# Two-layer hybrid decoder trunk on one core: the two channel blocks of each norm sum and layer norm sum are added on VectorE ahead of the product with the constant matrix

## The chip, the cores and the metric

The kernel runs on 1 core of one Trainium2 chip. The metric is device time in microseconds (us); lower is better. The engines are TensorE (PE in the profile, its weight loads PEld), VectorE (DVE), ScalarE (ACT), GpSimd (POOL) and SyncE (SP, which issues most DMAs).

## The reference

One sequence of 528 positions (512 and 16 meta tokens) with 1024 channels passes two layers. All arithmetic is float32. In each layer:

```python
def rms_norm(x, g):
    y = x * lax.rsqrt(jnp.mean(x * x, axis=-1, keepdims=True) + RMS_EPS)
    return y * g

def layer_norm(x, g, b):
    mu = jnp.mean(x, axis=-1, keepdims=True)
    var = jnp.mean(jnp.square(x - mu), axis=-1, keepdims=True)
    return (x - mu) * lax.rsqrt(var + LN_EPS) * g + b

def mixer_sublayer(h, ...):
    u = rms_norm(h, pre_g)
    q, k, v, f_logit, a_val, a_gate, sc_b, sc_c, sc_x = split(u @ w_in)
    y_attn = forgetting_attention(q, k, v, log_sigmoid(f_logit + b_forget))
    a = causal_depthwise_conv(a_val * sigmoid(a_gate), a_dw_w) + a_dw_b     # 31 taps, 256 channels
    y_conv = silu(layer_norm(a, a_ln_g, a_ln_b)) @ a_pw_w
    y_sc = sc_b * causal_depthwise_conv(sc_c * sc_x, sc_conv_w)             # 3 taps, 256 channels
    y = head_rms_norm(concat([y_attn, y_conv, y_sc]), head_g) @ w_out
    return h + rms_norm(y, post_g)

def ffn_sublayer(h, ...):
    g, up = split(causal_depthwise_conv(rms_norm(h, pre_g) @ w_up, conv_w))
    return h + rms_norm((silu(g) * up) @ w_down, post_g)
```

The change touches only sums over channels: the mean of squares of `rms_norm` over 1024 channels (both the pre norms and the post norms) and the two means of `layer_norm` over 256 channels.

## The kernel before

**Layout.** Activations lie with channels on the 128 partitions and positions along the free dimension: 1024 channels are 8 blocks of 128, and the 528 positions are worked on in two halves of 264 (H). In the second layer some spans are 250 or 256 columns, since the meta tokens fall away. A sum over channels is therefore a sum over the partitions and over the blocks. TensorE makes it: a product with a 128x128 constant matrix (`om_d`, all 1/1024; `om_c`, all 1/256) adds over the partitions and leaves the mean in every partition of one PSUM bank.

**Products.** The large matrix products are split in three: each float32 operand is a rounded high part and a low part of type fp32r, and `mm3` (line 831) makes high*high, high*low and low*high. Their weights stream in by DMA, ScalarE rounds the high part and VectorE subtracts for the low part (lines 652 and 653, 641 and 642, 666 and 667, 789 and 793). The products with `om_d` and `om_c` take plain float32 operands.

**A norm sum** (class `Norms`). `square` (line 916) is called for blocks k and k + 1 together: ScalarE squares a pair of blocks of n columns, 2n in all, and for k > 0 VectorE adds the pair to the pair `acc` (line 934), which stays two blocks wide. With `apart` set, the last pairs are not added but kept as parts of their own (line 937); that is so for the pre norm that ends layer 0 (`APART` = 2, line 2431), where pairs 4 and 6 are parts. At the end of the last layer, `square_alone` (line 944) keeps the last two blocks as single parts for the second half. `factor` (line 956) is a thread: it waits for each part, takes a PSUM bank and adds both blocks of a part into it on TensorE, one product a block (line 974). Then ScalarE and VectorE make the reciprocal root from the bank (lines 984 to 998).

Norm sums stand in four places: in the opening (two halves of the first pre norm); behind the output projection of each layer (post norm of the mixer and pre norm of the feed-forward part, two halves each); at the end of layer 0 (post norm, and the pre norm of layer 1 with its parts); and at the end of layer 1 (post norm alone).

**The layer norm** (`conv_tail`, line 1748) follows the 31 taps of the convolution (VectorE, line 1153). For each half TensorE multiplies `om_c` with both channel blocks of `conv` (line 1760), VectorE subtracts the mean (line 1764), ScalarE squares into `sq` (line 1766), TensorE multiplies `om_c` with both blocks of `sq` (line 1789), and `rsq` (line 1278) makes the factor.

**What sets the order.** A planner, `Flow` (line 253), writes each engine's instruction order by hand in the stretches around the mixers and the output norms. It keeps an estimated clock for each engine; operations carry an estimated duration, what they wait for, and a priority (a lower number goes first among those that are ready). TensorE's work consists of threads: generators that yield what they wait for, of which the first that is ready goes on. `flow.mm(us)` advances TensorE's estimated clock, and `mm4_us(264)` is 0.445 us for a float32 product, `dve_us(264)` 0.437 us for a VectorE operation. So each engine runs its queue in the planned order, whatever the true durations are. While `conv_tail` waits, TensorE's other threads are projections (`fill`), row maxima (`maxima`), exponentials and attention norms. In the feed-forward part the order is that of the program, and TensorE runs products (lines 837 and 2288) throughout.

Of the kernel before, what the change touches and what calls it, by code (L numbers as in the profile page):

```python
# [21 lines left out]
H = L // 2  # L22
# [25 lines left out]
LN_EPS = 1e-5  # L48
# [313 lines left out]
def mm4_us(n):  # L362

    return max(n / 600 + 0.005, 0.22)


def act_us(n):
    return 0.17 + 0.0009 * n


def dve_us(n):
    return 0.17 + 0.00101 * n
# [17 lines left out]
def tile_hybrid_trunk(ctx: ExitStack, tc: tile.TileContext, xT, wflat, pv_d, out):  # L390
    nc = tc.nc
# [58 lines left out]
    def const_mat(name, val, dt=F32):  # L450
        t = T(const, [P, P], dt, name)
        mset(t, val)
        return t
# [6 lines left out]
    om_c = const_mat("om_c", 1.0 / 256)  # L460
# [21 lines left out]
    flow = Flow()  # L482
# [5 lines left out]
    def half_sl(hf):  # L488
        return slice(H * hf, H * (hf + 1))
# [29 lines left out]
    sums = {}  # L519
# [172 lines left out]
    def dve(us, fn, *after, **kw):  # L692
        return flow.op("dve", us, fn, after, **kw)
# [204 lines left out]
    class Norms:  # L898
# [17 lines left out]
        def square(self, key, k, src, n, *after, prio=1):  # L916

            apart = self.alone.get(key, self.apart.get(key[0], 0))
            s = self.sums.setdefault(key, {"parts": {}})
            us = act_us(2 * n)  # L920
            box, slot = {}, Slot()

            def squares(tile):
                box["c"] = tile()
                nc.scalar.activation(box["c"], src, AF.Square)

            if k == 0:
                a = act(us, lambda: squares(lambda: T(self.pool, [P, 2, H], F32, "acc", 2)[:, :, :n]), *after,
                        prio=prio, takes=[(self.acc, slot)])
                s["acc"], s["at"] = box, a  # L930
            else:
                a = act(us, lambda: squares(lambda: self.c_tile(n)), *after, prio=prio, takes=[(self.c, slot)])
                if k < KD - 2 * apart:
                    s["at"] = dve(dve_us(2 * n), lambda: nc.vector.tensor_add(s["acc"]["c"], s["acc"]["c"], box["c"]),
                                  a, s["at"], prio=prio)
                    slot.close(s["at"])
            if k == 0 or k >= KD - 2 * apart:
                s["parts"][max(0, k // 2 - KD // 2 + apart + 1) if k else 0] = box, slot
                box["at"] = [a]
            if k == KD - 2 * apart - 2:  # L940
                s["acc"]["at"], s["acc"]["there"] = [s["at"]], True
            return a

        def square_alone(self, key, j, src, n, *after, prio=1):

# [179 lines left out]
    def mixer(l, ypool, first, close_first, spans, front, rzs, u_at):  # L1125
# [19 lines left out]
        conv, apads, gated_at, gated = front.conv, front.apads, front.at, front.gated  # L1145
# [10 lines left out]
        taps = []  # L1156
# [94 lines left out]
        def bank(kind):  # L1251

            slot = yield from flow.grab(banks[kind])
            return psum[:, slot.buf], slot
# [23 lines left out]
        def rsq(x, slot, eps, tok, prio=1):  # L1278

            mine = Slot()  # L1280
            box = {}
            us = act_us(H)
            prio = next(turns)

            def ln():
                box["r"], box["t"] = (T(mp, [P, H], F32, f"rs_{i}", 2) for i in "rt")
                nc.scalar.activation(box["r"], x, AF.Ln, bias=c_eps[eps] if eps else 0.0)

            a = act(us, ln, tok, prio=prio, takes=[(rings["rs"], mine)])
            b = act(us, lambda: nc.scalar.activation(box["r"], box["r"], AF.Exp, scale=-0.5), a, prio=prio)  # L1290
            c = act(us, lambda: nc.scalar.activation(box["t"], box["r"], AF.Square), b, prio=prio)
            d = dve(dve_us(H), lambda: nc.vector.scalar_tensor_tensor(
                box["t"], in0=x, scalar=eps, in1=box["t"], op0=ALU.add, op1=ALU.mult), c, prio=prio)
            slot.close(a, d)
            e = dve(dve_us(H), lambda: nc.vector.scalar_tensor_tensor(
                box["t"], in0=box["t"], scalar=3.0, in1=box["r"], op0=ALU.subtract, op1=ALU.mult), d, prio=prio)
            box["prio"] = prio
            return box, mine, e
# [449 lines left out]
        def conv_tail(blk):  # L1748

            w = blk.w  # L1750
            yield taps
            a2 = [ytiles(4), ytiles(5)]
            sq = [T(mq, [P, L + CK - 1], F32, "apad", 2) for _ in range(2)]
            us, vs = act_us(H), dve_us(H)
            at = {}
            for hf in range(2):
                c = half_sl(hf)
                ps, slot = yield from bank("mm")
                for j in range(2):
                    nc.tensor.matmul(ps[:, :H], lhsT=om_c, rhs=conv[j][:, c], start=j == 0, stop=j == 1)  # L1760
                tok = flow.mm(2 * mm4_us(H))
                subs = []
                for j in range(2):
                    subs.append(dve(vs, lambda j=j, ps=ps, c=c: nc.vector.tensor_sub(
                        conv[j][:, c], conv[j][:, c], ps[:, :H]), tok))
                    at[hf, j] = act(us, lambda j=j, c=c: nc.scalar.activation(sq[j][:, c], conv[j][:, c], AF.Square), subs[-1])
                slot.close(*subs)
                yield
            done = {}

            def silu(j, c, box, mine, e):
                n, s = conv[j][:, c], sq[j][:, c]
                f = dve(stt_us(H), lambda: nc.vector.scalar_tensor_tensor(
                    n, in0=n, scalar=gcol("a_ln_g", j), in1=box["t"], op0=ALU.mult, op1=ALU.mult), e)
                mine.use(f)
                g = act(us, lambda: nc.scalar.activation(s, n, AF.Exp, bias=minus_b[:, j:j + 1], scale=-1.0), f)
                g = act(us, lambda: nc.scalar.activation(s, s, AF.Ln, bias=c_one), g)
                g = act(us, lambda: nc.scalar.activation(s, s, AF.Exp, scale=-1.0), g)
                f = dve(stt_us(H), lambda: nc.vector.scalar_tensor_tensor(
                    n, in0=n, scalar=col("a_ln_b", j), in1=s, op0=ALU.add, op1=ALU.mult), g)  # L1780
                g = act(us, lambda: nc.scalar.copy(a2[j][0][:, c], n), f)
                return dve(vs, lambda: nc.vector.tensor_sub(a2[j][1][:, c], n, a2[j][0][:, c].bitcast(F32)), g)

            for hf in range(2):
                c = half_sl(hf)
                yield [at[hf, 0], at[hf, 1]]
                ps, slot = yield from bank("mm")
                for j in range(2):
                    nc.tensor.matmul(ps[:, :H], lhsT=om_c, rhs=sq[j][:, c], start=j == 0, stop=j == 1)
                box, mine, e = rsq(ps[:, :H], slot, LN_EPS, flow.mm(2 * mm4_us(H)))  # L1790
                done[hf] = [silu(j, c, box, mine, e) for j in range(2)]
                mine.close()
                yield
            yts, got = [], {}
            ends = done[0] + done[1]
            for m in range(2):
                yield ends
                yt = T(mq, [P, L], F32, "cacc", 2)
                for hf in range(2):
                    ps, slot = yield from bank("mm")  # L1800
                    mm3({hf: ps[:, :H]}, w, range(2), lambda b, k, hf: a2[k][b][:, half_sl(hf)],
                        cols=slice(P * m, P * (m + 1)))
                    tok = flow.mm(6 * mm_us(H))
                    got[m, hf] = act(us, lambda ps=ps, yt=yt, hf=hf: nc.scalar.copy(yt[:, half_sl(hf)], ps[:, :H]), tok)
                    slot.close(got[m, hf])
                    yield
                yts.append(yt)
            blk.slot.close(tok)
            for m in range(2):
                sq = T(mq, [P, L + CK - 1], F32, "apad", 2)[:, :L]  # L1810
                flow.thread(plain_head_norm(4 + m, yts[m], sq, [got[m, hf] for hf in range(2)]), True)
# [34 lines left out]
        for i, f in enumerate(sums_at(l, 1)):  # L1846
            copies, *adds = sum_steps(l, f)
            tok = flow.op("sp", 2.0, copies, (Tok(flow.pe + SUM_AT[i]),), prio=8, lat=SUM_LAT)
            for op in adds:
                tok = gp(SUM_US, op, tok, prio=8, lat=SUM_LAT)  # L1850
# [178 lines left out]
    with tc.tile_pool(name="pre", bufs=2, reuse_waits="tile") as sp, tc.manual_schedule(engines=every):  # L2029
# [13 lines left out]
        for k in range(KD):  # L2043
            hk, hi, lo, gc = h[:, k, :H], u_raw[0][k], u_raw[1][k], g0[:, k:k + 1]
            c = act(act_us(H) + 0.06, lambda hk=hk, hi=hi, gc=gc: nc.scalar.activation(hi, hk, AF.Copy, scale=gc),
                    h_at[0, k - k % 2], prio=0)
# [47 lines left out]
    for l in range(DEPTH):  # L2094
# [23 lines left out]
        with tc.tile_pool(name=f"fp{l}", bufs=2, reuse_waits="tile") as fp:  # L2118
# [226 lines left out]
            for part, nf in enumerate(PARTS):  # L2345
                for f in range(f0, f0 + nf):
# [15 lines left out]
                    for i in (2 * f, 2 * f + 1):  # L2362
# [6 lines left out]
                        ps = mmt((6, 2)[i % 2]) if ts else mmt()  # L2369
# [17 lines left out]
                if part < len(PARTS) - 1:  # L2387
# [3 lines left out]
                    for some in ((0, 1), *((m,) for m in range(2, KD))):  # L2391
                        ws = [next_w() for _ in some]
                        tiles = [mmt((4, 6, 2)[m % 3]) if seven else mmt() for m in some]
# [97 lines left out]
```

## Time and profile before

| | |
|---|---|
| runs | 1262.51, 1263.30, 1263.05 us; median 1263.05 |
| the profiled execution, first to last instruction (span) | 1262.4 us |
| mean granted TensorE clock in it | 0.999 |
| records on TensorE | 9554 matmuls |
| float32 products with `om_d` (line 974) | 84 records |
| float32 products with `om_c` (lines 1760 and 1789) | 16 + 16 records |
| HBM traffic over the span | 175 GB/s |

The profile gives the profiled execution's span; what lies around it is the rest of the measured time, 0.65 us up to the median. A row of the timeline shows the start, the length, the engine, the line, the operation with its tiles, its shape and how many such instructions follow one another; in brackets stands how long the engine was idle before it, and on which engine's instruction it waited. The lengths of matmul records overlap, so the pace of a run of matmuls is read from the chain of waits or from the starts. A row of the windows shows the stretch, its length, the busy time of TensorE, of its weight loads, of VectorE, ScalarE and GpSimd (with instructions), then the clock, the share of the DMA engines and GB/s. A row of a source view shows the shortest, median and longest duration in ns.

### The profile page before, as it was taken

The numbers are of one execution on the slowest core, as the hardware profiler recorded it, in microseconds if no ns is written. First come the engines' busy times: TensorE is split into PE (matmuls) and PEld (weight loads), VectorE is DVE, ScalarE is ACT, GpSimd is POOL, SyncE is SP. The second block draws the span as 40 slices with busy tenths as digits, with TensorE's granted clock in tenths as the row PEclk, the third lists the DMA queues.
The fourth block names the chain that finished last, engine by engine and source line by source line (L and its number), as shares of the span: only waits on it lengthen the run. The fifth ranks groups of instructions, "written<-read, shape, count | busy, mean of one in ns | idle before, by whom it ended". The sixth has DMA issues, their size and how long they took to land.

```text
span 1262.4 us, 24292 instructions
## 1 busy us (share of the span) xinstructions
PE 1243.7 (99%) x9554; PEld 1194.0 (95%) x9554; DVE 926.1 (73%) x1581; ACT 710.3 (56%) x1377; POOL 174.6 (14%) x360
## 2 busy tenths in 40 slices
PE   8999999999999999999999999999999999999997
PEld 8998898999999999999999988999999899989997
DVE  7887866589874776487688878656799748756964
ACT  7254576655444663476673545775554447526763
POOL 1323411001111001010003244120021000000000
PEclk9999999999999999999999999999999999999999
DMA  7357551726648755776652584547166565465611
GB/s 245 82 155 173 126 119 44 259 87 149 186 147 334 244 193 149 240 195 169 208 189 67 156 194 110 144 111 241 71 163 176 146 218 170 153 223 182 203 60 67
DMA packets 80755, 206.59 MB, mean 164 GB/s; under 512 B 8624, under 2 KB 18992, under 8 KB 80128
## 3 DMA queue, kind: packets, MB, share of 16 engines
q1 hardware_dynamic: 66976, 168.20, 42.1%
q0 software_dynamic: 13664, 36.84, 13.0%
q8 instruction: 75, 1.23, 0.4%
q14 instruction: 40, 0.33, 0.1%
HBM read 170.82 MB, written 50.60 MB: 175 GB/s over the span
## 4 chain that ended last, share of the span: by engine, by line
PE 89%; DVE 3%; issue 3%; DMA 2%; ACT 2%; POOL 1%; SPq 0%; DVEq 0%; POOLq 0%; ACTq 0%
PE psum L837 58%; PE psum L2288 17%; PE psum L1407 5%; PE psum L1671 3%; PE psum L1637 2%; PE psum L974 1%; PE psum L1593 1%; DMA raw<-in_w_dram 1%; PE psum L1737 1%; PE psum L1323 1%; DMA w_split<-slo 0%; DMA h<-in_w_dram 0%; POOL dm L1608 0%; DVE yp L1050 0%; DMA h<-in_x_dram 0%
## 5 line engine op out<-in xcount | busy, mean ns | idle before, releaser
L837 PE MATMUL psum<-y,whi 128*128 128x264 f32 (+3 forms) x1968 | 383.8, 299 | 0.8 <-DVE zs L989 0.7
L837 PEld LDWEIGHTS psum<-y,whi 128*128 128x128 f32 x1968 | 305.6, 188 | 13.8 <-DVE zs L989 0.9
L837 PE MATMUL psum<-uhi,whi 128*128 128x264 f32 (+1 forms) x1168 | 292.1, 289 | 1.5 <-ACT uhi L2069 0.7
L837 PE MATMUL psum<-ulo,whi 128*128 128x264 f32 (+1 forms) x1168 | 285.7, 284 | 0.6 <-DVE ulo L2071 0.4
L837 PE MATMUL psum<-uhi,wlo 128*128 128x264 f32 (+1 forms) x1168 | 285.1, 283 | 0.0
L837 PE MATMUL psum<-y,wlo 128*128 128x264 f32 (+3 forms) x984 | 273.7, 297 | 0.3 <-DVE wlo L793 0.3
L837 PEld LDWEIGHTS psum<-uhi,whi 128*128 128x128 f32 x1168 | 201.5, 188 | 6.2 <-issue 1.6
L837 PEld LDWEIGHTS psum<-ulo,whi 128*128 128x128 f32 x1168 | 201.6, 188 | 1.3 <-DVE ulo L2071 0.6
L837 PEld LDWEIGHTS psum<-uhi,wlo 128*128 128x128 f32 x1168 | 201.3, 188 | 0.0
L837 PEld LDWEIGHTS psum<-y,wlo 128*128 128x128 f32 x984 | 177.8, 188 | 5.8 <-DVE wlo L793 0.6
L2173 DVE SCALAR_TENSOR_TENSOR c<-zs,pv,c 128x528 f32<-128x528 f32 (+1 forms) x176 | 130.6, 756 | 23.5 <-ACT c L2171 22.2
L652 ACT CAST whi<-raw 128x1024 fp32r<-128x1024 f32 (+1 forms) x65 | 66.1, 1020 | 97.1 <-PE psum L837 74.5
L793 DVE TENSOR_TENSOR wlo<-raw,whi 128x1024 fp32r<-128x1024 f32 (+2 forms) x80 | 95.6, 1203 | 29.7 <-ACT whi L789 29.2
L789 ACT CAST whi<-raw 128x1024 fp32r<-128x1024 f32 (+2 forms) x80 | 81.7, 1031 | 24.9 <-PE psum L837 18.0
L653 DVE TENSOR_TENSOR wlo<-raw,whi 128x1024 fp32r<-128x1024 f32 (+1 forms) x65 | 76.9, 1183 | 21.1 <-ACT whi L652 21.0
L1153 DVE SCALAR_TENSOR_TENSOR cacc<-apad,pv,cacc 128x528 f32<-128x528 f32 x120 | 87.6, 772 | 0.1
L2288 PE MATMUL psum<-uhi,whi 128*128 128x258 f32 (+1 forms) x252 | 71.3, 284 | 0.0
L2288 PE MATMUL psum<-ulo,whi 128*128 128x258 f32 (+1 forms) x252 | 71.2, 283 | 0.0
L2288 PE MATMUL psum<-uhi,wlo 128*128 128x258 f32 (+1 forms) x252 | 70.7, 283 | 0.0
L2171 ACT ACTIVATE c<-zs,pv 128x528 f32<-128x528 f32 (+1 forms) x88 | 63.0, 727 | 6.8 <-DVE zs L2136 2.7
L2206 POOL COPY cols<-y 128x1 f32<-128x1 f32 x24 | 17.2, 716 | 335.8 <-ACT y L2187 335.5
L2288 PE MATMUL psum<-t,shi 128*128 128x258 f32 (+1 forms) x336 | 63.2, 283 | 0.0
(273 smaller groups left out, 2323.9 us busy)
## 6 DMA issues: line engine op xcount, KB each, us to landing
raw<-in_w_dram SPq DMA_DIRECT2D x114, 512.0 KB, 4.5
raw<-in_w_dram SPq DMA_DIRECT2D x30, 448.0 KB, 5.1
h<-in_w_dram SPq DMA_DIRECT2D x25, 512.0 KB, 4.5
raw<-w_sum SPq DMA_DIRECT2D x21, 512.0 KB, 5.4
h<-w_sum SPq DMA_DIRECT2D x21, 512.0 KB, 4.8
h<-in_w_dram POOLq DMA_DIRECT2D x16, 512.0 KB, 4.6
w_sum<-h POOLq DMA_DIRECT2D x16, 512.0 KB, 6.4
w_sum<-in_w_dram SPq DMA_DIRECT2D x26, 256.0 KB, 5.2
```

The costliest lines, as they stand in the source:

```text
L652: nc.scalar.copy(hi[:, :sz], raw[:, :sz])
L653: last_low[0] = nc.vector.tensor_sub(lo[:, :sz], raw[:, :sz], hi[:, :sz].bitcast(F32))
L789: nc.scalar.copy(box["hi"][:, :sz], box["raw"][:, :sz])
L793: nc.vector.tensor_sub(lo[:, :sz], box["raw"][:, :sz], box["hi"][:, :sz].bitcast(F32))
L837: nc.tensor.matmul(d, lhsT=w[a][:, k, cols], rhs=rhs(b, k, hf), start=start and i == 0 and p == 0, stop=stop and i == n - 1 and p == 2)
L1153: nc.vector.scalar_tensor_tensor(conv[j], in0=src, in1=conv[j], scalar=col("a_dw_w", CK * j + i), op0=ALU.mult, op1=ALU.add)
L1407: nc.tensor.matmul(ps[:n, :nw], lhsT=(uhi, ulo)[ui][:, k, P * b:P * b + n], rhs=w[wi][:, k % 4, :], start=k == 0 and p == 0, stop=k == KD ...
L1637: nc.tensor.matmul(s, lhsT=k[:, ka:ka + kn], rhs=q[:, s0:qz], start=i == 0, stop=i == 1)
L1671: nc.tensor.matmul(acc[:, s0 - qa:qz - qa], lhsT=vals[:, b].rearrange("p h d -> p (h d)")[:, o:o + P], rhs=box["p"], start=b == 0, stop=b ...
L2171: nc.scalar.activation(dst, src[:, 2:2 + 2 * fw], AF.Copy, scale=wtap(2, t))
L2173: nc.vector.scalar_tensor_tensor(dst, in0=src[:, i:i + 2 * fw], scalar=wtap(i, t), in1=dst, op0=ALU.mult, op1=ALU.add)
L2288: nc.tensor.matmul(psum[:, bank, :n7], lhsT=w[a][:, k0 + k, :], rhs=rhs(b, k), start=start and k == 0 and p == 0, stop=stop and k == K2 - ...
```

## The change

Ahead of each product with `om_d` on a pair of blocks, a new VectorE operation `fold` adds the second block to the first in place, and the product reads the first alone (`box["tiles"] = (0,)`, which `factor` looks up). That holds for `acc`, once its last pair is added, and for the pairs kept apart; the single blocks of `square_alone` stay as they are. In `conv_tail`, `both` adds the two blocks of `conv` into `sq[0]` for each half, and later the two blocks of `sq` in place; one product with `om_c` is left of two. The planner counts half of the earlier TensorE time for each. In `square` and `conv_tail`:

```diff
@@ -936,10 +936,16 @@
                     slot.close(s["at"])
             if k == 0 or k >= KD - 2 * apart:
                 s["parts"][max(0, k // 2 - KD // 2 + apart + 1) if k else 0] = box, slot
-                box["at"] = [a]
+                box["at"] = [self.fold(box, n, prio, a)] if k else [a]
             if k == KD - 2 * apart - 2:
-                s["acc"]["at"], s["acc"]["there"] = [s["at"]], True
+                s["acc"]["at"], s["acc"]["there"] = [self.fold(s["acc"], n, prio, s["at"])], True
             return a
+
+        def fold(self, box, n, prio, *after):
+
+            box["tiles"] = (0,)
+            return dve(dve_us(n), lambda: nc.vector.tensor_add(box["c"][:, 0, :], box["c"][:, 0, :], box["c"][:, 1, :]),
+                       *after, prio=prio)
 
         def square_alone(self, key, j, src, n, *after, prio=1):
 
@@ -1753,12 +1759,17 @@
             sq = [T(mq, [P, L + CK - 1], F32, "apad", 2) for _ in range(2)]
             us, vs = act_us(H), dve_us(H)
             at = {}
+
+            def both(t, c, after):
+                return dve(vs, lambda: nc.vector.tensor_add(sq[0][:, c], t[0][:, c], t[1][:, c]), *after)
+
+            sums = [both(conv, half_sl(hf), taps) for hf in range(2)]
             for hf in range(2):
                 c = half_sl(hf)
+                yield [sums[hf]]
                 ps, slot = yield from bank("mm")
-                for j in range(2):
-                    nc.tensor.matmul(ps[:, :H], lhsT=om_c, rhs=conv[j][:, c], start=j == 0, stop=j == 1)
-                tok = flow.mm(2 * mm4_us(H))
+                nc.tensor.matmul(ps[:, :H], lhsT=om_c, rhs=sq[0][:, c], start=True, stop=True)
+                tok = flow.mm(mm4_us(H))
                 subs = []
                 for j in range(2):
                     subs.append(dve(vs, lambda j=j, ps=ps, c=c: nc.vector.tensor_sub(
@@ -1781,13 +1792,13 @@
                 g = act(us, lambda: nc.scalar.copy(a2[j][0][:, c], n), f)
                 return dve(vs, lambda: nc.vector.tensor_sub(a2[j][1][:, c], n, a2[j][0][:, c].bitcast(F32)), g)
 
+            sums = [both(sq, half_sl(hf), [at[hf, 0], at[hf, 1]]) for hf in range(2)]
             for hf in range(2):
                 c = half_sl(hf)
-                yield [at[hf, 0], at[hf, 1]]
+                yield [sums[hf]]
                 ps, slot = yield from bank("mm")
-                for j in range(2):
-                    nc.tensor.matmul(ps[:, :H], lhsT=om_c, rhs=sq[j][:, c], start=j == 0, stop=j == 1)
-                box, mine, e = rsq(ps[:, :H], slot, LN_EPS, flow.mm(2 * mm4_us(H)))
+                nc.tensor.matmul(ps[:, :H], lhsT=om_c, rhs=sq[0][:, c], start=True, stop=True)
+                box, mine, e = rsq(ps[:, :H], slot, LN_EPS, flow.mm(mm4_us(H)))
                 done[hf] = [silu(j, c, box, mine, e) for j in range(2)]
                 mine.close()
                 yield
```

## The prediction

> **What bounds the kernel now.** I read the page first, then the chain of waits in order of time, then the source view of the three lines whose products are halved, then the timeline around each place where they stand. The page's rows for the span, for the engines and for the chain by engine:
>
> ```profile
> span 1262.4 us, 24292 instructions
> PE 1243.7 (99%) x9554; PEld 1194.0 (95%) x9554; DVE 926.1 (73%) x1581; ACT 710.3 (56%) x1377; POOL 174.6 (14%) x360
> ...
> PE 89%; DVE 3%; issue 3%; DMA 2%; ACT 2%; POOL 1%; SPq 0%; DVEq 0%; POOLq 0%; ACTq 0%
> ```
>
> TensorE is the bound: it lies idle for 1262.4 - 1243.7 = 18.7 us in all, and 89% of the chain is its own matmuls. VectorE has 336 us free over the span, though not evenly. A TensorE microsecond taken away should therefore shorten the run by about as much, except where TensorE goes on to wait for another engine. The chain of waits in order of time (start, length, engine, line, instructions) gives what a product costs TensorE when the next follows at once:
>
> ```profile
> 162.50 1.78 PE psum L1760 x8
> ...
> 165.01 0.89 PE psum L1789 x4
> ...
> 247.66 0.89 PE psum L974 x4
> ...
> 277.08 107.95 PE psum L837 x886
> ...
> 874.00 0.84 PE psum L974 x4
> ...
> 1235.88 0.86 PE psum L974 x4
> ```
>
> The source views of the three lines, with the instructions counted:
>
> ```profile
> L974 PE MATMUL psum<-acc,om_d x64: 372/385/461, 18.0 to 1248.2; 128*128 128x264 f32 x48, 128*128 128x250 f32 x8, 128*128 128x256 f32 x8
> ...
> L974 PE MATMUL psum<-c,om_d x20: 379/386/483, 636.1 to 1251.8; 128*128 128x264 f32 x16, 128*128 128x256 f32 x4
> ...
> L1760 PE MATMUL psum<-cacc,om_c x16: 384/386/386, 162.3 to 792.0; 128*128 128x264 f32 x16
> ...
> L1789 PE MATMUL psum<-apad,om_c x16: 383/386/387, 164.8 to 796.7; 128*128 128x264 f32 x16
> ```
>
> Line 1760 runs for two layers, two halves and two channel blocks, 8 products, and shows 16 records: a float32 product is two records. Four records take 0.89 us of the chain at 264 columns, so a product costs 2 x 0.2225 = 0.445 us (not the 0.385 us that one record lasts, since records overlap), 0.42 us at 250 columns and 0.43 us at 256. The ordinary split products of line 837 step at 107.95 / 886 = 0.122 us.
>
> **What is removed.** Every pair of products on one accumulated tile becomes one. Of line 974's 64 records with `acc`, half go (24 + 4 + 4); of its 20 with `c`, the 16 of 264 columns come from the two layer-0 pre-norm halves, whose last four blocks are kept apart, and 8 go; the 4 of 256 columns are the single blocks that end the kernel (line 944) and stay. Lines 1760 and 1789 lose 8 each. That is 56 records, 28 products: 24 of 264 columns, 2 of 250, 2 of 256, or 24 x 0.445 + 2 x 0.42 + 2 x 0.43 = 12.4 us of TensorE's time.
>
> The Trainium skill, page "TensorE: Matmul & The Clock Gate", section "Back-to-back issue gap", gives a warm matmul N / 2.4 + 2.5 ns, 112.5 ns at 264 columns; the split products' 0.122 us is near that, the float32 records' 0.2225 us is not. By that rule 56 records would be worth an estimated 6.3 us and not 12.4; the rows decide for 12.4, and what the smaller price would mean is a rival below.
>
> **What is added.** 28 VectorE additions of two 264-wide float32 blocks in SBUF. None is in the trace; the nearest rows are products of two such tiles (VectorE, opening), with the idle time before one of them in brackets:
>
> ```profile
> 25.95 0.43 DVE L989 SCALAR_TENSOR_TENSOR rs<-psum,rs 128x264 f32<-128x264 f32 x1 [0.77 <-ACT rs L988]
> ...
> 27.70 0.43 DVE L1119 TENSOR_TENSOR sccx<-sccx,rz 128x264 f32<-128x264 f32 x1 [0.17 <-ACT sccx L1117]
> 28.06 0.43 DVE L1119 TENSOR_TENSOR cxp<-cxp,rz 128x264 f32<-128x264 f32 x1
> ```
>
> One lasts 0.43 us and the next starts 0.36 us later, so a fold is bounded by 0.36 us (in a full queue) and 0.43 us (as latency). 28 of them are 10 to 12 us of VectorE. In the chain of one norm the fold's 0.43 us stands where a product's 0.445 us is taken out, so a factor comes at about the same time as before; what changes is that TensorE does other work in that half microsecond. Hidden cover: everything else TensorE has queued. Where TensorE has nothing else, the product is lost to a wait. So I go place by place.
>
> **Opening, 2 products.** TensorE's timeline:
>
> ```profile
> 17.99 1.13 PE L974 MATMUL psum<-acc,om_d 128*128 128x264 f32 x4 [0.47 <-DVE acc L934]
> ...
> 23.38 1.05 PE L974 MATMUL psum<-acc,om_d 128*128 128x264 f32 x4
> ...
> 30.69 0.39 PE L837 MATMUL psum<-uhi,whi 128*128 128x264 f32 x1 [0.72 <-ACT uhi L2069]
> 31.45 0.39 PE L837 MATMUL psum<-ulo,whi 128*128 128x264 f32 x1 [0.37 <-DVE ulo L2071]
> ```
>
> The first product already waits 0.47 us for VectorE's sum, and at 30.69 and 31.45 TensorE has caught up with the second half's normalised input. Being 0.89 us earlier there only lengthens that wait: I count these two at nothing. The two folds (0.7 us) stand on a full VectorE queue, but ahead of its 0.77 us gap at 25.95, which takes them; without that cover they would cost up to 0.7 us.
>
> **Convolution tail, 8 products (4 a layer).** TensorE's windows (length, then TensorE busy), then VectorE's rows there:
>
> ```profile
> 160.00:215.00 55.00, 54.57 (x392) 49.27 (x391) 35.42 (x91) 41.42 (x109) 9.85 (x25) 1.00 0.32 83
> 215.00:280.00 65.00, 65.00 (x523) 64.47 (x523) 46.37 (x78) 40.22 (x78) 0.20 (x4) 1.00 0.51 173
> ...
> 870.00:907.00 37.00, 36.12 (x288) 35.16 (x287) 29.23 (x54) 21.32 (x44) 0.00 (x0) 1.00 0.42 144
> ```
>
> ```profile
> 156.54 2.24 DVE L1153 SCALAR_TENSOR_TENSOR cacc<-apad,pv,cacc 128x528 f32<-128x528 f32 x3
> 162.71 0.43 DVE L1545 SCALAR_TENSOR_TENSOR pair_lo<-psum,pair_hi 128x264 fp32r<-128x264 f32 x1 [3.93 <-ACT pair_hi L1542]
> ...
> 164.11 1.22 DVE L793 TENSOR_TENSOR wlo<-raw,whi 128x1024 fp32r<-128x1024 f32 x1
> ```
>
> VectorE is idle for 3.93 us between the last convolution tap and this, so the folds of the means cost nothing. Those of the squares may find a weight split of 1.22 us ahead of them; the branch then comes about a microsecond later, while TensorE runs projections and attention (54.57 of 55 us busy). What waits behind a fold is the next split and the next evacuation of a bank. The 8 x 0.445 = 3.6 us count in full.
>
> **Output norms of layer 0, 4 products, and its pre-norm region, 8.** From 215 to 280 us TensorE is busy 65.00 of 65.00: full credit, 1.8 us. The 8 products between 620 and 656 us also stand in a stream; the one wait behind them is
>
> ```profile
> 659.58 0.51 PE L837 MATMUL psum<-y,whi 128*128 128x264 f32 x2 [0.70 <-DVE zs L989]
> ```
>
> and it is for the factor that follows the last of these products, so chain and TensorE move together and the 0.70 us stay. Credit 3.6 us.
>
> **Output norms of layer 1, 4 products.** TensorE and then VectorE:
>
> ```profile
> 886.59 1.05 PE L974 MATMUL psum<-acc,om_d 128*128 128x264 f32 x4
> 894.50 1.01 PE L974 MATMUL psum<-acc,om_d 128*128 128x250 f32 x4
> 901.79 0.39 PE L837 MATMUL psum<-uhi,whi 128*128 128x264 f32 x1 [0.52 <-ACT uhi L1066]
> 902.43 0.39 PE L837 MATMUL psum<-ulo,whi 128*128 128x264 f32 x1 [0.25 <-DVE ulo L1068]
> ```
>
> ```profile
> 888.77 0.68 DVE L934 TENSOR_TENSOR acc<-acc,c 128x500 f32<-128x500 f32 x1 [0.84 <-ACT c L925]
> ```
>
> After that gap VectorE works without a pause worth naming until TensorE's waits at 901.79 and 902.43, which are for its row and ScalarE's. The products at 886.59 and 894.50 (0.445 + 0.42 us) only make TensorE arrive sooner at that wait, and the fold at 894 puts 0.36 us into VectorE's full row. The products at 874 and after 902 count: 0.87 us credit, 0.36 us cost.
>
> **End, 2 products.** TensorE is fed until its last output products; then
>
> ```profile
> 1250.51 0.42 DVE L1899 TENSOR_TENSOR yp<-yp,psum 128x256 f32<-128x256 f32 x1 [3.37 <-PE psum L837]
> ...
> 1251.43 0.70 PE L974 MATMUL psum<-c,om_d 128*128 128x256 f32 x2 [0.96 <-ACT c L950]
> ```
>
> Both removed products run before 1250.5 us and their folds have 3.37 us of idle VectorE ahead of the last chain: 0.86 us credit.
>
> **Sum.** 3.56 + 1.78 + 3.56 + 0.87 + 0.86 = 10.6, less 0.36: 10.3 us off the profiled 1262.4 us, 1252.1 us. The median of the runs (1263.05 us) lies 0.65 us above that span, so the time is 1252.8 us.
>
> **The rivals.** First, half the gain goes into the mixers. Their order is planned from estimated times, so shorter products and 28 new VectorE entries reorder attention, too. TensorE's waits there now:
>
> ```profile
> PE psum L1617 <- POOL dm L1608: 1.4, 2, 1.0
> ...
> PE psum L1593 <- issue: 1.2, 1, 1.2
> PE psum L1593 <- DMA k<-pair_hi: 1.1, 1, 1.1
> ...
> PE psum L1323 <- ACT q L1619: 0.8, 2, 0.4
> ...
> PE psum L1671 <- POOL pf L1651: 0.6, 2, 0.3
> ```
>
> They are 5.1 us; as much again would leave 10.3 - 5.1 = 5.2 us, 1257.9 us. For it speaks that these waits hang on small latencies; against it that a new order can as well remove one. Second, the float32 record's 0.2225 us is not stream time that TensorE gets back, and 56 records return only the 0.122 us of the split rows: 12.4 shrinks to 6.8 us, the credit to 5.5 us, 1257.6 us. Against it: the row of eight records at 162.50 steps as the rows of four do. That is what the skill's rule would come to, on this kernel's own rows. Third, nothing moves: the branches that the products feed are the bound everywhere, and each fold's 0.43 us replaces 0.445 us; 1263 us. The 65.00 of 65.00 speaks against it. Fourth, slower: on VectorE's queue, which runs in order, the folds of the 20 norm products fall behind a weight split (1.22 us, row 164.11), and the product stands at the head of TensorE's queue meanwhile. All 20 so placed cost 24.4 - 12.4 = 12.0 us: 1275 us. It decides from a mean stall of 12.4 / 28 = 0.44 us a product on. The 0.47 us at 17.99 shows that it exists; against it, it occurs at one place. That the change does not do what it says would show as records not halved; planner and code leave little room for that, and it is in the third case's chance.
>
> **How the numbers follow.** Forecast 0.66, first rival 0.18, second 0.04, third 0.05, fourth 0.07. A measurement here can tell about 0.2% (2.5 us) from no change; so faster 0.66 + 0.18 + 0.04 = 0.88, same 0.05, slower 0.07. The forecast alone reaches from full credit (12.4 us, 1250.6 us) to the opening's folds uncovered and a microsecond more of waits (1254.5 us); with a microsecond below for waits that vanish, and the first two rivals taken in above with some excess, the range is 1249.5 to 1259.5 us.
>
> **What would show it.** Right: line 974 with 32 + 12 = 44 records, the two `om_c` lines with 8 each, TensorE busy some 12 us less, 28 new additions of 0.43 us, the waits at 30 and 902 us longer by 0.9 us each, the stretch from 215 to 280 us still without idle time and shorter by 1.8 us. Wrong: new TensorE waits at line 974 for VectorE (fourth rival), longer waits at lines 1593 and 1617 (first), or TensorE's busy time falling by some 7 us (second).

## The result, and the profile after

The changed kernel takes 1271.95 us (median of 4 runs, 1270.96 to 1276.06) against 1262.94 us for the kernel before beside it: a ratio of 1.0078, 95% interval 1.0061 to 1.0094. It is 9.0 us slower where 10.3 us less was forecast. The profiled execution took 1271.82 us, with a span of 1270.1 us, so 1.7 us lie around the span here; the 0.65 us used ahead set the span of one execution against the median of others.

The page of the changed kernel, span and engines:

```profile
span 1270.1 us, 24213 instructions
PE 1239.9 (98%) x9498; PEld 1187.5 (93%) x9498; DVE 936.0 (74%) x1609; ACT 709.1 (56%) x1377; POOL 177.7 (14%) x360
```

TensorE has its 56 records fewer and VectorE its 28 additions more. But TensorE's busy time falls by 3.8 us instead of 12.4, and its idle time rises from 18.7 to 1270.1 - 1239.9 = 30.2 us. The source views of the lines that the change touches (records, their length in ns as least, median and most, first and last start):

```profile
L980 PE MATMUL psum<-acc,om_d x32: 372/385/461, 19.5 to 1257.1; 128*128 128x264 f32 x24, 128*128 128x250 f32 x4, 128*128 128x256 f32 x4
...
L1800 PE MATMUL psum<-apad,om_c x8: 386/386/490, 168.9 to 802.5; 128*128 128x264 f32 x8
...
L947 DVE TENSOR_TENSOR acc<-acc x16: 417/427/435, 18.9 to 1255.2; 128x264 f32<-128x264 f32 x12, 128x250 f32<-128x250 f32 x2, 128x256 f32<-128x256 f32 x2
```

So the change did what it says, and one addition lasts the 0.43 us that was forecast. What is new stands in the view of TensorE's waits (in total, times, longest):

```profile
PE psum L1623 <- DVE rs_t L1298: 3.7, 2, 1.8
PE psum L837 <- ACT uhi L2080: 2.8, 1, 2.8
PE psum L837 <- ACT uhi L1072: 2.2, 2, 1.2
PE psum L837 <- DVE zs L995: 2.1, 1, 2.1
PE psum L1800 <- DVE pair_lo L1551: 1.9, 2, 0.9
```

The first and the fifth did not exist. The second was 0.72 us, the third 0.52 us (once), the fourth 0.70 us. A product that waits for its own addition, the fourth rival's sign, is not among them: that row comes to 0.3 us.

The first and the fifth, both new, lie in the mixers, once in each layer. TensorE's timeline of layer 0, changed kernel, without the projection products:

```profile
164.75 0.61 PE L1771 MATMUL psum<-apad,om_c 128*128 128x264 f32 x2
165.56 0.61 PE L1771 MATMUL psum<-apad,om_c 128*128 128x264 f32 x2
168.94 1.16 PE L1800 MATMUL psum<-apad,om_c 128*128 128x264 f32 x4 [0.95 <-DVE pair_lo L1551]
...
195.09 0.39 PE L1623 MATMUL psum<-dm,ones_r 128*128 128x264 f32 x1
195.32 1.05 PE L1329 MATMUL psum<-apad,bd 128*128 128x264 f32 x4
198.22 0.36 PE L1623 MATMUL psum<-dm,ones_r 128*128 128x264 f32 x1 [1.85 <-DVE rs_t L1298]
```

The same places in the kernel before:

```profile
164.85 1.05 PE L1789 MATMUL psum<-apad,om_c 128*128 128x264 f32 x4
167.95 1.05 PE L1789 MATMUL psum<-apad,om_c 128*128 128x264 f32 x4
...
198.17 0.29 PE L1617 MATMUL psum<-dm,ones_r 128*128 128x264 f32 x1
...
201.82 0.28 PE L1617 MATMUL psum<-dm,ones_r 128*128 128x264 f32 x1
```

Before, the variance products of the two halves stood 3.1 us apart, and the last head's two products with `ones_r` 3.65 us apart, with other work between and no wait. In the changed kernel the variance products stand together and wait for a bank, and between the last head's two products stand only four records, so TensorE waits 1.85 us for the bank. That is another order of the work, not a longer piece of it. The planner made it from the changed estimates. VectorE's timeline shows what holds the bank at 168.94:

```profile
166.89 0.43 DVE L1764 TENSOR_TENSOR apad<-apad,apad 128x264 f32<-128x264 f32 x1
167.23 1.22 DVE L793 TENSOR_TENSOR wlo<-raw,whi 128x1024 fp32r<-128x1024 f32 x1
168.45 0.43 DVE L1551 SCALAR_TENSOR_TENSOR pair_lo<-psum,pair_hi 128x264 fp32r<-128x264 f32 x1
```

The operation that reads the bank out and so frees it (line 1551) is queued behind an addition (line 1764) and a weight split (line 793). e5 below has the same wait without the addition, so the addition is not needed for it.

### The profile page after: what moved, and what is told of

It reads as the page before. It is cut to its first block, busy times and chain, and to the rows that moved or that the text cites. A ratio compares the mean times of both kernels' runs of the same rounds, so it can differ in the third digit from the quotient of the medians.

```text
span 1270.1 us, 24213 instructions
## 1 busy us (share of the span) xinstructions
PE 1239.9 (98%) x9498; PEld 1187.5 (93%) x9498; DVE 936.0 (74%) x1609; ACT 709.1 (56%) x1377; POOL 177.7 (14%) x360
## 4 chain that ended last, share of the span: by engine, by line
PE 84%; DVE 7%; issue 3%; DMA 2%; ACT 2%; POOL 1%; DVEq 0%; SPq 0%; POOLq 0%; ACTq 0%
PE psum L837 55%; PE psum L2299 17%; PE psum L1413 5%; PE psum L1677 3%; PE psum L1643 2%; DVE yp L1056 1%; PE psum L1599 1%; DVE h L1066 1%; DMA raw<-in_w_dram 1%; DVE acc L934 1%; PE psum L1743 1%; DVE wlo L793 1%; DVE ulo L1074 1%; PE psum L1329 0%; DMA w_split<-slo 0%
## 5 line engine op out<-in xcount | busy, mean ns | idle before, releaser
L2217 POOL COPY cols<-y 128x1 f32<-128x1 f32 x24 | 21.7, 903 | 326.3 <-ACT y L2198 326.2
```

## The experiments

Two causes were set against each other: the new order of the work (A), and the additions in VectorE's queue (B). A third, that a removed product returns little (C), was the prediction's second rival.

**Products and additions in the order of the kernel before (e1, e2).** The planner is told what it was told before, so that every engine keeps its order. In e1 each addition is issued right behind the operation that completes its operands, and one product stands where the first of two stood. e2 has the one product and no addition. The core of e1:

```diff
                 nc.scalar.activation(box["c"], src, AF.Square)
+                if k >= KD - 2 * apart:
+                    fold(box)
...
-                tok = flow.mm(len(tiles) * mm4_us(n))
+                tok = flow.mm((1 if "alone" in box else 2) * mm4_us(n))
...
-                for j in range(2):
-                    nc.tensor.matmul(ps[:, :H], lhsT=om_c, rhs=sq[j][:, c], start=j == 0, stop=j == 1)
+                nc.tensor.matmul(ps[:, :H], lhsT=om_c, rhs=sq[0][:, c], start=True, stop=True)
```

> All 28 additions and halved products, but the planner is told nothing of them (it still counts two products and no addition), so that every engine keeps the order of the kernel before, with the additions put in. Theory A (the new order is what costs: the products themselves return what the prediction counted): 1252 to 1256 us. Theory B (the additions in VectorE's queue cost, in whatever order): 1268 us or more. Theory C (a removed product returns little of its 0.445 us): 1258 to 1264 us.

> The order of the kernel before, one product instead of two in all 28 places and no addition: the second channel block is left out of every such sum, so the sums are incomplete and only the time is of use. Theory A and theory B: 1251 to 1253 us, the full worth of the products. Theory C: 1257 us or more. The difference to the run with the additions in the same order is what the 28 additions cost: theory A under 3 us, theory B over 15 us.

e1 took 1263.86 us, a ratio of 1.0008 (0.9998 to 1.0017). e2 took 1252.98 us, 0.9926 (0.9911 to 0.9941). The products alone return 9.7 us: C is out. TensorE's busy time falls by 11.8 us in e2 (1243.7 to 1231.9), the 12 that the prediction named. The additions take 10.9 us back, even in the old order. That difference was to be under 3 us by A and over 15 us by B; it lies between, so neither holds alone.

**One part of the change, planned as in the change (e3, e4).** e3 switches the additions of the norm sums off (`norms.folds` becomes false) and keeps the layer norm's; e4 is the reverse. The core of e3:

```diff
+FOLDS = ('ln',)
...
-                box["at"] = [self.fold(box, n, prio, a)] if k else [a]
+                box["at"] = [self.fold(box, n, prio, a)] if k and self.folds else [a]
...
+        norms.folds = "open" in FOLDS
```

> Only the layer norm's 8 additions and 8 products of the change, planned as in the change; the norm sums are as before. Theory A: the mixers are replanned by this part, so most of the loss is here: 1264 to 1270 us. Theory B: 8 of 28 additions, so 8/28 of a loss of 9 us: 1265 to 1266 us. Theory C: 1263 us.

> Only the norm sums' 20 additions and 20 products, planned as in the change; the layer norm is as before. Theory A: the opening's 1.6 us loss stays, the rest returns its products since the mixers are planned nearly as before: 1255 to 1260 us. Theory B: 20 of 28 additions: 1269 us. Theory C: 1263 to 1266 us.

The layer norm's part alone took 1272.63 us, 1.0077 (1.0062 to 1.0092), the norm sums' part alone 1265.88 us, 1.0021 (1.0007 to 1.0036). The layer norm's part, with the order that the planner makes for it, is enough for the whole loss; e7 below shows that its eight additions by themselves are not. Both came out slower than theory A had them, e4 above 1255 to 1260 us by some 6 us: the norm sums' part did not return its products either.

**Old or new order, each with and without the work (e5, e6).** The change's plan, but the additions issue nothing; e5 issues one product of two, e6 both.

```diff
-            return dve(dve_us(n), lambda: nc.vector.tensor_add(box["c"][:, 0, :], box["c"][:, 0, :], box["c"][:, 1, :]),
+            return dve(dve_us(n), lambda: None,
```

> The change's own order of work, with one product of two and no additions at all (the second channel block is left out of each sum, as in the run with the old order): beside that run, at 1253.0 us, only the order differs. Theory A (the new order costs by itself, about 8 us, whoever does the sums): 1260 to 1263 us. Theory B (the new order is as good as the old one, and it is the additions in VectorE's queue that cost): 1251 to 1255 us.

> The change's order of work, but with both products of each sum and no additions, so that the work is that of the kernel before. Theory A: about 8 us over the kernel before, 1269 to 1273 us. Theory B: 1261 to 1265 us.

e5 took 1270.73 us, 1.0056 (1.0040 to 1.0072), and e6 1280.54 us, 1.0131 (1.0112 to 1.0150). With the kernels above this makes a table of medians in us:

| work | order of before | order of the change | the order costs |
| --- | --- | --- | --- |
| two products, no additions | 1263.4 | 1280.5 | 17.1 |
| one product, no additions | 1253.0 | 1270.7 | 17.7 |
| one product and the additions | 1263.9 | 1272.0 | 8.1 |

This is theory A, at about twice its price. The order costs 17.1 us with the old work and 17.7 with the halved one (a factor of 1.013 either way by the ratios). In the new order the additions add little: 1.2 us by the medians, 2.8 us by the ratios, whose intervals overlap. They are hidden there in an order in which TensorE waits in any case. The costs of the additions and of the order are therefore no separate terms. Both together take 19.0 us (1272.0 - 1253.0): 10.9 us for the additions and 8.1 us for the order on top of them, or 17.7 us for the order and about 1.2 us for the additions. e5's waits are the changed kernel's, without a single addition:

```profile
PE psum L1623 <- DVE rs_t L1298: 3.7, 2, 1.8
PE psum L837 <- ACT uhi L2080: 3.2, 1, 3.2
PE psum L837 <- DVE zs L995: 2.0, 1, 2.0
...
PE psum L1800 <- DVE pair_lo L1551: 1.9, 2, 0.9
```

Where it is lost can be read in part from the gates of the FFN. The source view of that activation (44 of them over both layers, first and last start), in e2 and then in e5:

```profile
L2190 ACT ACTIVATE c<-c x44: 617/642/657, 283.5 to 1198.6; 128x528 f32<-128x528 f32 x22, 128x512 f32<-128x512 f32 x22
```

```profile
L2194 ACT ACTIVATE c<-c x44: 614/642/656, 296.6 to 1215.3; 128x528 f32<-128x528 f32 x22, 128x512 f32<-128x512 f32 x22
```

At the first gate e5 is 13.1 us behind, at the last 16.7 us, though both issue the same products. Part of the 13.1 us is work done earlier: by then TensorE has 2152 matmul records behind it in e5 and 2121 in e2.

**The layer norm's part in the old order (e7), and the additions on GpSimd (e8).** e7 is e1 without the norm sums' lines; e8 is e1 with another engine:

```diff
-                nc.vector.tensor_add(box["c"][:, 0, :], box["c"][:, 0, :], box["c"][:, 1, :])
+                nc.gpsimd.tensor_add(box["c"][:, 0, :], box["c"][:, 0, :], box["c"][:, 1, :])
```

> Only the layer norm's part of the change (8 additions, 8 products fewer), in the order of the kernel before. Theory A: the same part planned anew took 1272.6 us, and nearly all of that was the order, so here 1261 to 1265 us. Theory B: the additions cost in any order, so 1270 to 1274 us.

> All additions in the order of the kernel before, but on GpSimd, which is busy for 14% of the span, so that VectorE's queue is as it was. If what the additions cost in the old order (10.9 us) is the time that they hold in VectorE's queue ahead of other work, 1253 to 1257 us. If it is that each product now stands at the head of TensorE's queue until its addition is done, no less than with VectorE: 1263 us or more, by as much as a GpSimd addition is longer.

e7 took 1263.87 us, 1.0001 (0.9992 to 1.0011), where the same part planned anew had taken 1272.63: theory A again. e8 took 1268.86 us, 1.0038 (1.0025 to 1.0052). Two of the four groups of its additions, by line (busy us, mean ns):

```profile
L931 POOL TENSOR_TENSOR acc<-acc 128x264 f32<-128x264 f32 (+2 forms) x16 | 17.7, 1106 | 316.7 <-DVE acc L934 316.7
L1772 POOL TENSOR_TENSOR apad<-apad,apad 128x264 f32<-128x264 f32 x4 | 3.9, 976 | 5.9 <-ACT apad L1770 5.9
```

With VectorE's queue as it was before, the longer addition makes it 5.0 us slower than e1. e1's waits:

```profile
PE psum L1805 <- DVE apad L1772: 2.3, 2, 1.2
PE psum L984 <- DVE acc L931: 2.3, 4, 0.9
...
PE psum L837 <- DVE zs L999: 1.3, 1, 1.3
...
PE psum L837 <- ACT uhi L1076: 1.2, 1, 1.2
```

The products wait 4.9 us for their additions in e1 (2.3, 2.3 and 0.3 us by the same view) and 10.7 us in e8 (7.0, 2.3, 1.0 and 0.4 us). The 5.8 us between are most of the 8.0 us between the two profiled spans. So in the old order the additions cost by their length in the chain from the squares to the factor, as far as the waits show it, and not by holding VectorE. Of the 8.7 us between the profiled spans of e1 and e2, 5.4 are idle time of TensorE (25.0 against 19.6); the other 3.3 are busy time (1235.2 against 1231.9), for which no view gives a reason.

**The work of before in other orders (e9, e16, e17), and the halved work replanned (e10).** Nothing that is computed changes in the first three, only a figure that the planner is told:

```diff
-    return 0.17 + 0.00101 * n
+    return 0.18 + 0.00101 * n
```

That is e9; e16 has 0.16, and e17 has 0.05 us for `HOP` instead of 0.06. e10 is planned for one product and no addition.

> The kernel before with all its work, two products for each sum and no additions; only the planner is told 0.01 us more for each VectorE operation. That moves 385 of 7047 listed TensorE instructions, and the planner's own clock at the end of what it plans goes from 655.0 to 664.8 us (the change: 671.1; its layer norm part alone: 668.6; its norm sums alone: 659.2; measured, these three stand 9.0, 9.6 and 2.6 us over the kernel before). Theory A1 (any order other than the tuned one costs several us, whatever the work, and the planner's clock shows it): 1267 to 1272 us. Theory A2 (the loss comes of the additions standing in the layer norm's chain, and a plan without them stays good): 1261 to 1265 us.

> One product of two and no additions (the second channel block is left out of each sum), planned anew for just that work: 28 products fewer and nothing added, yet the planner's own clock ends at 654.8 us, as before (655.0). Theory A1: the new plan eats the whole saving, 1260 to 1265 us. Theory A2: as with the old order, 1251 to 1255 us.

> The kernel before with all its work; the planner is told 0.01 us less for each VectorE operation (e9 was told 0.01 us more and took 1271.9 us). The planner's own clock ends at 652.7 us, before the 655.0 of the kernel before; 353 of 7047 listed TensorE instructions move. If the order of the kernel before is one good order among many and any other costs: 1266 to 1273 us. If the loss needs a plan that is longer by its own clock: 1260 to 1264 us.

> The same with another figure: the planner is told 0.05 us for a hop between engines instead of 0.06. Its clock ends at 653.6 us; 304 listed TensorE instructions move. Any other order costs: 1266 to 1273 us. Only a longer plan costs: 1260 to 1264 us.

e9 took 1271.86 us, 1.0069 (1.0054 to 1.0084); e16 1266.24 us, 1.0027 (1.0017 to 1.0037); e17 1265.26 us, 1.0017 (1.0008 to 1.0026). e10 took 1265.55 us, 1.0015 (1.0002 to 1.0028), 12.6 us more than the same work in the old order. Five other orders of the same or less work were measured here (e6 is the fifth), and each was slower than the kernel before, by 2.3 to 17.1 us. The order of the kernel before is better than any of them, and each edit measured here that made the planner leave it paid for that. e9 came out in the range of A1 and e10 0.6 us above it; e16 lies at the lower end of the first of its two ranges, e17 between its two.

**Another order for the whole change (e11).** The change with four figures of the planner changed, so that its own clock ends earlier than for the kernel before.

```diff
-    HOP = 0.06
+    HOP = 0.04
...
-    return 0.17 + 0.00101 * n
+    return 0.15 + 0.00101 * n
```

> All of the change's work, additions included, but with other figures for the planner alone (0.04 us for a hop instead of 0.06, 0.15 instead of 0.17 us for the fixed part of a VectorE operation, 0.002 us more for a float32 product, the norm additions 0.2 later in priority), chosen because the planner's own clock then ends at 652.5 instead of 671.1 us. Theory A1 (the order is what cost): 18.6 us shorter in the plan should give 9 to 12 us, 1259 to 1263 us, no slower than before. If the additions cost in every order, 1268 to 1273 us as with the change.

It took 1270.66 us, 1.0060 (1.0045 to 1.0075): 1.3 us better than the change, which is not clear of the scatter, where 9 to 12 were expected. That is the range set for additions that cost in every order, but e11's order is new as well, so it cannot tell the two causes apart. It does show that a plan shorter by the planner's own clock need not be a faster kernel. e16 and e17 say the same: shorter by that clock, and slower.

**The clock after a wait (e12).**

```diff
+    def idle(n):
+        for _ in range(n):
+            nc.tensor.matmul(psum[:, 7, 400:512], lhsT=om_c, rhs=om_c[:, :112], start=True, stop=True)
...
+                    idle(8 * (hf and hd == HEADS - 1))
                     nc.tensor.matmul(ps[:, :H], lhsT=ones_r, rhs=dm[:, c], start=True, stop=True)
```

> The change as it is, with idle products (112 columns of the constant matrix by itself, into columns of PSUM that nobody reads) standing ahead of three products that wait: 12 where TensorE waited 2.85 us at 32.33 us, 8 each where it waited 1.85 us at 198.22 and 830.99 us. They do no work and should end within the wait. If the waits also cost a halved clock afterwards (the granted clock of the change's runs was 0.992 to 0.997, some 4 to 10 us), the mean clock rises to 0.997 or more and the time falls by 2 to 4 us, 1268 to 1270 us. If only the waits themselves count, no change, 1271 to 1273 us.

It took 1269.44 us, 1.0049 (1.0033 to 1.0066), 2.5 us less than the change by the medians, as was expected of a halved clock; but the interval overlaps the change's own, 1.0061 to 1.0094. The mean granted clock over the four runs rose from 0.9953 to 0.9975, nearly half of it for one run of the change at 0.992. The time that the lower clock costs, estimated as (1 - clock) times the span, falls from 6.0 to 3.2 us, about the gain. The two profiled executions do not bear it out: both have a clock of 0.997. e12 keeps it at the three filled places and loses it at two others, 0.83 over 660 to 670 us and over 910 to 920 us. So it is not shown that the filled waits gave the gain. The idle products fit into the waits, as TensorE's timeline of e12 shows (two records a product):

```profile
29.10 2.83 PE L848 MATMUL psum<-om_c 128*128 128x112 f32 x24
32.10 0.39 PE L837 MATMUL psum<-uhi,whi 128*128 128x264 f32 x1 [0.17 <-ACT uhi L2085]
...
195.37 1.94 PE L848 MATMUL psum<-om_c 128*128 128x112 f32 x16
197.38 0.36 PE L1628 MATMUL psum<-dm,ones_r 128*128 128x264 f32 x1
```

**Issuing the product later (e13, e14, e15).** e13 is e1 without the layer norm's lines. In e14 and e15 each product that has an addition is put off until four or eight further products are issued.

```diff
+    def mm_(*a, **k):
+        nc.tensor.matmul(*a, **k)
+        for x in put_off:
+            x[0] -= 1
+        while put_off and put_off[0][0] <= 0:
+            put_off.popleft()[1]()
```

> Only the norm sums' part (20 additions, 20 products fewer), in the order of the kernel before, the one product where the first of the two stood. With both parts in that order the additions took back 10.9 of 9.7 us. If they cost by making each product wait at the head of TensorE's queue, they cost here as well: 1261 to 1264 us. If it is VectorE's time, with 20 of 28 additions about as much: 1260 to 1263 us, and the next two kernels no better.

> As the one before, but each of the products that have an addition is issued behind the next four projection products (4 x 0.122 = 0.49 us, where its second product used to end), so that the addition (0.43 us) runs while TensorE works. If the cost was the product at the head of TensorE's queue, most of the products' credit (20 x 0.445 = 8.9 us, less what is paced by a transfer) appears: 1256 to 1260 us, faster than both kernels. If the cost is VectorE's time or the later factor, no better than the one before.

> The same with eight projection products ahead (0.98 us) or as many as the first reader of the sum leaves. If an addition often stands behind a weight split (1.22 us) in VectorE's queue, better than with four by some tenths for each: 1255 to 1259 us; if four were enough, the factors come later and it is a little slower than with four.

They took 1263.02 us, 1.0004 (0.9993 to 1.0014); 1262.47 us, 1.0000 (0.9988 to 1.0011); and 1262.47 us, 1.0007 (0.9997 to 1.0017). All three are the kernel before, within what can be measured. Three of e14's waits, where line 404 issues the products that are put off:

```profile
PE psum L397 <- ACT uhi L2097: 1.3, 1, 1.3
PE psum L397 <- DVE zs L1017: 1.3, 1, 1.3
PE psum L404 <- DVE acc L948: 1.3, 2, 0.7
```

The wait for the sums' additions at the head of TensorE's queue was 2.2 us in e13. It is 1.3 us in e14 and 0.9 us in e15, and the time does not fall with it beyond the scatter. So standing there is not the whole cost. Some of it comes back further on, where TensorE waits for what the factor scales: the wait for `uhi` was 0.9 us in e13, the one for `zs` 1.3 us already. Where the rest comes back, no view shows.

No kernel with all of the work beat the kernel before. For the layer norm's products the putting off was not tried: their readers follow at once in the plan.

## Why the prediction was wrong

**Removed: right in size.** The credit was 10.6 us place by place, of 12.4. e2 measures 9.7 us, with TensorE's busy time down by 11.8. The 0.445 us a product was read rightly from the chain, and the estimate of 6.3 us by the rule of the Trainium skill, page "TensorE: Matmul & The Clock Gate", section "Back-to-back issue gap", was too small.

**The step that failed first: the additions' cover.** The prediction said that an addition stands where a product is taken out, "so a factor comes at about the same time as before; what changes is that TensorE does other work in that half microsecond". The first half, where it holds, denies the second: TensorE waits for the addition, or for the factor behind it, and does no other work in that time. The prediction saw that in the opening and at two products of layer 1, and credited all other places. In the old order (e1) TensorE waits for the additions at credited places, too: 1.15 us in the convolution tail of each layer (at 164.58 and 791.36 us), 0.29 and 0.73 us in the region of layer 1's pre norm (at 635.55 and 638.46 us). With the order held fixed the additions cost 10.9 us, not 0.36. For the convolution tail, credited with 3.6 us "in full", e7 measures nothing gained.

**The other step that failed: the order.** The sum has no term for it. The first rival names it, at 5.1 us and as a part of the gain. Its waits rose about as it said, from 5.1 us to 9.0 us at the same lines in the changed kernel, but e5 and e6 price the order at 17 us by itself, and e1 leaves 8.1 us for it on top of the additions. The sizing took the waits that the mixers had as a measure of what a new order could add, and most of the cost lies elsewhere. e9, e16 and e17 show that other plans cost even with nothing changed in the work. Nothing in the profile of before gave that price.

**The waits that "only lengthen".** The opening's wait did grow from 0.72 to 2.85 us, more than the 0.89 us counted, and the one for `zs` from 0.70 to 2.1 us, where it was to stay. They were counted as free of further cost. The windows below show that they need not be: a wait can be followed by a halved clock, at 1.7 us each time. By the mean clocks that is an estimated 5 us of the loss (6.0 us for the changed kernel's four runs, 1.3 us in the profiled execution of the kernel before, at 0.999). Which waits bring it on is not shown.

**The other rivals.** The second is out by e2. The fourth comes nearest in time (1275 us), but not by its mechanism in the changed kernel, where the row of products that wait for an accumulated sum's addition comes to 0.3 us; in the old order (e1) it is there, 2.3 us for the norms and 2.3 us for the layer norms. The third, each addition replacing a product with nothing moved, gives the time that e1, e7 and e13 to e15 measure: that is where the change ends in the old order.

**What it named as signs.** 44 records, 8 in each `om_c` line, 28 additions of 0.43 us, and 0.86 us of credit at the end (the changed kernel's lag shrinks from 8.5 us at the last FFN gate to 7.7 us at the span's end): right. TensorE busy 12 us less: 3.8, and 11.8 in e2. The waits at 30 and 902 us longer by 0.9 us each: by 2.1 us, and by 0.5 us (0.98 us at 910.99). The stretch from 215 to 280 us without idle time: it now ends in a wait of 1.19 us at 281.58.

**Open.** Of the 13.3 us between the spans of e6 and of the kernel before, 9.3 are idle time of TensorE (28.0 against 18.7) and about 1.3 the lower clock (0.998 against 0.999); the rest lies in records that take longer, and no view says why. e9 has it too: its profiled span is 6.1 us longer at the same clock, with 3.4 us more idle time. Whether an order exists in which the change gains is open: two planned for it were measured, besides that of the kernel before.

## What to carry to other kernels

Where a planner or a scheduler derives the order from estimated costs, an edit changes two things; hold the order fixed in one experiment, and give the new order the old work in another, before the edit itself is judged. An operation that replaced another in the chain to a stage's first operand saved nothing there, however idle its engine was: count the chain, not the engine. A wait of TensorE can cost more than its length, since a halved clock can follow it.

## What the runs showed of the hardware

A wait of 1.2 to 1.9 us can halve TensorE's clock for some 3.4 us. The windows of the changed kernel (length, TensorE busy, granted clock, then the DMA columns), around its waits at 198.22 and 281.58:

```profile
195.30:198.20 2.90, 1.07 (x5) 1.00 0.01 3
198.20:201.60 3.40, 3.38 (x11) 0.54 0.00 0
201.60:205.00 3.40, 3.34 (x16) 0.96 0.00 0
...
278.00:281.30 3.30, 2.25 (x15) 1.00 0.31 125
281.60:285.00 3.40, 3.09 (x16) 0.82 0.78 320
285.00:288.40 3.40, 3.40 (x22) 0.68 0.00 0
```

Each such halving costs 1.7 us, as the windows add up (3.4 x 0.46 + 3.4 x 0.04, and 3.4 x 0.18 + 3.4 x 0.32), about as much as the wait itself. It does not follow every wait: the 2.85 us at 32.33 and the 1.85 us at 830.99 of the same execution had none. Nor does it belong to a place: e5 has the first wait in the same order of work, 1.84 us at 198.10, and keeps its clock there,

```profile
190.00:200.00 10.00, 7.45 (x44) 1.00 0.06 22
200.00:210.00 10.00, 9.94 (x60) 1.00 0.00 1
```

while e3 has it, 1.85 us at 197.43, with a clock of 0.91 and 0.92 over these two windows. In e12 this place, with the wait filled, keeps its clock, but since e5 keeps it unfilled, this one execution does not show that the filling did it:

```profile
190.00:200.00 10.00, 9.22 (x57) 1.00 0.01 4
200.00:210.00 10.00, 9.94 (x63) 1.00 0.01 2
```

The Trainium skill, page "TensorE: Matmul & The Clock Gate", section "HAM oscillation — how this bites in real kernels", warns of idle gaps over about 3.4 us; here shorter ones were enough, and the measurement decides. The Trainium skill, page "TensorE: Matmul & The Clock Gate", section "What's actually happening", has the activity judged in free-running windows of about 3.4 us; the length of the halved stretch agrees, and so does it that like waits are not followed alike.

The same addition of two 264-column blocks took 0.43 us on VectorE and, by the means of its lines, 0.73 to 1.1 us on GpSimd (e8).
